# Last two tiles of the output in three token pieces, with 1 / rms from a square root and one Newton step

## The chip, the cores and the metric

The kernel runs on one core of one Trainium2 chip. The metric is the device time of one execution in microseconds (us), lower being better; the number that counts is the median over several runs. The core has five engines that run on their own and wait for one another by semaphores: TensorE (PE, with its weight loads shown apart as PEld), VectorE (DVE), ScalarE (ACT), GpSimd (POOL) and SyncE (SP), which here only issues DMAs. The profile is of one execution; "span" is the time from its first to its last instruction.

## The reference

One inference step of a two-layer decoder trunk on 544 tokens: 512 of a new sequence and 32 (8 sequences of 4) that continue from states. Layer 0 mixes tokens with a Mamba-2 recurrence, layer 1 with HGRN2; each is followed by a squared-ReLU MLP, and every sub-layer has an RMSNorm ahead of it. The change lies in the last lines of this:

```python
def rmsnorm(x, w):
    xf = x.astype(jnp.float32)
    y = xf * lax.rsqrt(jnp.mean(xf * xf, axis=-1, keepdims=True) + EPS)
    return (y * w.astype(jnp.float32)).astype(x.dtype)

def squared_relu_mlp(u, w_up, w_down):
    return jnp.square(jax.nn.relu(u @ w_up)) @ w_down
...
        h = h + squared_relu_mlp(rmsnorm(h, norm_mlp_w[layer]), mlp_w_up[layer], mlp_w_down[layer]).astype(h.dtype)
    y = rmsnorm(h, norm_f_w)
```

So the last thing computed is the down projection of the second MLP (4096 to 1024 channels), its addition to the residual, and the final norm, which needs for each token the sum of squares over all 1024 channels.

## The kernel before

**Layout.** Activations lie with channels on the 128 partitions and tokens along the free dimension: `x` is eight tiles of 128 channels by 544 tokens. [...] Weights are split into a high part (rounded to the type float32r) and a low part (the remainder), activations likewise, and a product of 128 channels by 128 channels is three matmuls: high by high, high by low, low by high. Each matmul instruction comes with its own weight load. A few small products work on plain float32; the trace shows two matmul instructions for each of them.

**The last MLP.** `mlp` goes through a list of units. Most of the down projection comes from a scheme that forms seven products instead of eight; the last two output tiles of the last quarter (channel tiles 6 and 7) are left over, and `finish` computes them together with the final norm. Its operands are `ops`, eight activation tiles split in high and low (`gh`, `gl`), and two units of weights `w` (`whi`, `wlo`), which `split` casts on ACT (L200) and subtracts on DVE (L201).

**What `finish` does,** for each half h of 272 tokens:

1. For tile 6 and then tile 7, 24 matmuls (8 operands, 3 each) into the half's bank of an accumulator (L1464, `pd`).
2. The sum is added to `x` on DVE (L1468), squared on ACT (L1469), and multiplied by the norm's weight column on DVE into `xw` (L1472). The squares of tiles 0 to 6 are gathered in `ssq` (L1474); tile 7's stay in `sq`.
3. The sums over channels: the tokens are cut in three chunks of 91 (the last overlaps), and each chunk of `ssq` and of `sq` is the stationary operand of a product with a column of ones (L1479, `fn_pc`). The result has tokens on partitions, 91 by 3.
4. `newton` (L351 to L363) on DVE: mean and epsilon (L1481), a first guess of 1 / sqrt from the bits of the float (L357), minus half the mean (L358), then three Newton steps of three instructions each (L360 to L362).
[...]
[...]

`newton` is also called by the other norms of the kernel (`rstd_steps`, and the HGRN2 heads); they call it without the new argument.

**What sets the order.** A planner in the compiler puts each engine's instructions in an order: among those that its own costs hold to be ready, the one that stands first in the program. So `fn_pc` and `fn_pr` of the first half stand in PE's queue between matmuls of the second half, and each engine then takes its queue strictly in that order, waiting where an operand is late. A DMA that ACT issues stands in ACT's queue and waits there for the `y` that it sends.

**Buffers.** [...] `f_pool` holds two buffers each of `sq`, `rb` and `y`. ACT evaluates functions from a table set that must be loaded first: the kernel warms it with an `Exp` of a small tile `warm` at its start.

Of the kernel before, what the change touches and what calls it, by code (L numbers as in the profile page):

```python
# [9 lines left out]
F32 = mybir.dt.float32  # L10
F32R = mybir.dt.float32r
I32 = mybir.dt.int32
AF = mybir.ActivationFunctionType
ALU = mybir.AluOpType
ADD, SUB, MUL, MAX, MIN = ALU.add, ALU.subtract, ALU.mult, ALU.max, ALU.min

P = 128
D = 1024
KT = D // P
# [3 lines left out]
HF = T // 2  # L23
SEQS = 8
EPS = 1e-5
# [79 lines left out]
def trunk(ctx: ExitStack, tc: tile.TileContext, io):  # L105
    nc = tc.nc
# [12 lines left out]
    x = [xa[:, k] for k in range(KT)]  # L119
    vec = const.tile([P, N_VEC], F32, name="vec")  # L120
    ident = const.tile([P, P], F32, name="ident")
    ones = const.tile([P, 2], F32, name="ones")
    nc.vector.memset(ones, 1.0)
    warm = const.tile([P, 2], F32, name="warm")
# [8 lines left out]
    ssq = const.tile([P, T], F32, name="ssq")  # L133
    nc.gpsimd.memset(ssq, 0.0)
    nt = ctx.enter_context(tc.tile_pool(name="nt", bufs=2))
# [183 lines left out]
    def block(w, c):  # L319

        return w[c // 512][:, c % 512 : c % 512 + P]
# [22 lines left out]
    def mx(name):  # L344
        return psm.tile([P, 512], F32, tag="mx", name=name)
# [2 lines left out]
        return t.rearrange("p (a b) -> p a b", a=2)  # L348


    def newton(ms, n):  # L351

        p = ms.shape[0]
        r = nt.tile([P, n], F32, tag="nwr", name="nwr")[:p]
        t = nt.tile([P, n], F32, tag="nwt", name="nwt")[:p]
        m = nt.tile([P, n], F32, tag="nwm", name="nwm")[:p]
        nc.vector.tensor_scalar(r.bitcast(I32), ms.bitcast(I32), -0.5, 1597463007.0, MUL, ADD)  # L357
        nc.vector.tensor_scalar(m, ms, -0.5, None, MUL)  # L358
        for _ in range(3):
            nc.vector.tensor_tensor(t, r, r, MUL)  # L360
            nc.vector.tensor_tensor(t, t, m, MUL)
            nc.vector.scalar_tensor_tensor(r, t, 1.5, r, ADD, MUL)  # L362
        return r  # L363

    def rstd_steps(scale, name, res, where, wait):

        pc = mx(f"{name}_pc")
        for c in range(5):
            c0 = min(c * P, T - P)
            nc.tensor.matmul(pc[:, c : c + 1], ssq[:, c0 : c0 + P], ones[:, 0:1], start=True, stop=True)  # L370
        ms = nt.tile([P, 5], F32, tag="ms", name=f"{name}_ms")
        nc.vector.tensor_scalar(ms, pc[:, :5], scale, EPS, MUL, ADD)
        r = newton(ms, 5)
        yield wait
        pr = mx(f"{name}_pr")
        pr2 = mx(f"{name}_pr2")
        for c in range(5):
            dst, w = (pr[:, c * P : (c + 1) * P], 0) if c < 4 else (pr2[:, :NS], P - NS)
            nc.tensor.matmul(dst, r[:, c : c + 1].to_broadcast([P, P]), ident[:, w:], start=True, stop=True)
        rb = where.tile([P, T], F32, tag="rb", bufs=1, name=f"{name}_rb")  # L380
        nc.scalar.copy(rb[:, :NP_], pr)
        nc.scalar.copy(rb[:, NP_:], pr2[:, :NS])
        res.append(rb)
# [30 lines left out]
    def weighted(k):  # L414
        xw.append(pers.tile([P, T], F32, tag=f"uh{k}", name=f"xw{k}"))
        return xw[k]
# [550 lines left out]
    def mlp(name, plan, v0, then, last=False):  # L967
# [158 lines left out]
        for x_ in plan:  # L1126
# [10 lines left out]
            elif x_[0] == "d":  # L1137
                _, u, k0, k1, m, q = x_
                if k0 == 0:
                    if q == 0 and m == 0:  # L1140
                        drain(name)
                        background(split_sums(), name, wait=2)
                    acc[m] = [acc_tile(f"pd{q}_{m}"), None]
                    if last and q == MLP_GROUPS - 1 and m >= KT - 2:
                        if m == KT - 2:
                            continue
                        ops = [g[u - 8 - m + i] for i in range(8)]
                        ws.close()
                        finish([unit(u - 1), unit(u)], ops, [acc[KT - 2][0], acc[m][0]])
                        continue  # L1150
                    acc[m][1] = unit(u)
                else:
                    ahead()
                ps, w = acc[m]
                gb = u - 8 - m
                products(ps, w, [g[gb + k] for k in range(k0, k1)], k0 == 0, k1 == 8, k0 * P)
                release((k0 < 4 <= k1) + (k1 == 8))
                if k1 == 8:
                    add_to_x(m, ps, then if q == MLP_GROUPS - 1 else None)
            else:  # L1160
                if queues[0] and queues[0][0][2] == name:
                    drain(name)
                seventh(*x_)
# [4 lines left out]
    def hgrn(then):  # L1168
# [151 lines left out]
        def states(h, d):  # L1320
# [41 lines left out]
            for c in range(4):  # L1362
# [12 lines left out]
            nc.vector.tensor_reduce(ms, o2, mybir.AxisListType.X, ADD)  # L1375
            nc.vector.tensor_scalar(ms, ms, 1.0 / P, EPS, MUL, ADD)
            r = newton(ms, 5)
            nc.vector.tensor_tensor(
                o2[:, :4], po.rearrange("p (a b) -> p a b", b=P), r[:, :4].unsqueeze(2).to_broadcast([P, 4, P]), MUL
# [68 lines left out]
                    add_to_x(2 * mp + i, ps, then if half == 1 else None)  # L1448
        es.close()

    CH = (0, 91, HF - 91)

    def finish(w, ops, pss):

        es = ExitStack()
        pool = es.enter_context(tc.tile_pool(name="f_pool", bufs=2, reuse_waits="tile"))
        ms2 = (KT - 2, KT - 1)
        for h in range(2):
            hs = slice(h * HF, (h + 1) * HF)
            sqs = []  # L1460
            for m, (hi, lo), ps in zip(ms2, w, pss):
                for k, (oh, ol) in enumerate(ops):
                    for j, (a, o) in enumerate(((hi, oh), (hi, ol), (lo, oh))):
                        nc.tensor.matmul(  # L1464
                            ps[:, h, :HF], block(a, k * P), o[:, hs], start=(k == 0 and j == 0), stop=(k == len(ops) - 1 and j == 2)
                        )
                sq = pool.tile([P, HF], F32, tag=f"sq{m}", name=f"sq{m}_{h}")
                nc.vector.tensor_tensor(x[m][:, hs], ps[:, h, :HF], x[m][:, hs], ADD)  # L1468
                nc.scalar.activation(sq, x[m][:, hs], AF.Square)  # L1469
                if h == 0:  # L1470
                    weighted(m)
                nc.vector.tensor_scalar(xw[m][:, hs], x[m][:, hs], vec[:, V_NF + m : V_NF + m + 1], None, MUL)  # L1472
                sqs.append(sq)
            nc.vector.tensor_tensor(ssq[:, hs], ssq[:, hs], sqs[0], ADD)  # L1474
            sq = sqs[1]
            pc = mx(f"fn_pc{h}")
            for n, c in enumerate(CH):
                for i, t in enumerate((ssq[:, hs], sq)):
                    nc.tensor.matmul(pc[:91, n : n + 1], t[:, c : c + 91], ones[:, 0:1], start=(i == 0), stop=(i == 1))  # L1479
            ms = nt.tile([P, 5], F32, tag="ms", name=f"fn_ms{h}")[:91, :3]  # L1480
            nc.vector.tensor_scalar(ms, pc[:91, :3], 1.0 / D, EPS, MUL, ADD)  # L1481
            r = newton(ms, 3)
            pr = mx(f"fn_pr{h}")
            for n, c in enumerate(CH):
                nc.tensor.matmul(pr[:, c : c + 91], r[:, n : n + 1].to_broadcast([91, P]), ident[:91, :91], start=True, stop=True)
            rb = pool.tile([P, HF], F32, tag="rb", name=f"fn_rb{h}")
            nc.scalar.copy(rb, pr[:, :HF])
            y = pool.tile([P, KT, HF], F32, tag="y", name=f"y{h}")
            for k in (0, 5, 1, 6, 2, 7, 3, 4):
                xk = xw[k][:, hs]  # L1490
                if k < 5:
                    nc.vector.tensor_tensor(y[:, k], xk, pr[:, :HF], MUL)
                else:
                    nc.gpsimd.tensor_tensor(y[:, k], xk, rb, MUL)
            for i, (k0, k1) in enumerate(((0, 2), (5, 7), (2, 5), (7, 8))):
                (nc.scalar if k0 >= 5 else nc.sync).dma_start(io["yT"][k0:k1, :, hs].rearrange("k p t -> p k t"), y[:, k0:k1])
        es.close()
# [117 lines left out]
def _build(arrays):  # L1615
    import concourse.bacc as bacc

    nc = bacc.Bacc("TRN2", target_bir_lowering=False, num_devices=1)
    io = {n: nc.dram_tensor(f"in_{n}", v.shape, mybir.dt.from_np(v.dtype), kind="ExternalInput").ap() for n, v in arrays.items()}
    for n, s in _OUT.items():  # L1620
        io[n] = nc.dram_tensor(f"out_{n}", s, F32, kind="ExternalOutput").ap()
    with tile.TileContext(nc) as tc:
        trunk(tc, io)
    return nc
# [22 lines left out]
```

## Time and profile before

| what | value |
|---|---|
| time, median of 3 runs | 1528.34 us (1526.07 to 1529.8) |
| the profiled execution's own time | 1524.65 us |
| its span | 1522.7 us |
| PE busy | 1503.0 us, 99% of the span |
| DVE, ACT, POOL busy | 1230.8, 842.2, 149.6 us |
| granted TensorE clock, mean | 0.995 of full |

The span is 1.95 us shorter than the time of the same execution; the rest lies outside the first and the last instruction. PE is busy almost throughout, and the only long stretch in which it isn't is the end: the last slice of the forty in the page's view of the span is the one with little PE work in it. A row of the timeline reads: start, duration, engine, line, operation, output from inputs, sizes (partitions by free elements), and in brackets how long the engine stood idle before it and who ended that.

### The profile page before, as it was taken

To read this page: it belongs to the slowest core of one execution; us is meant where nothing else is said; L and a number is where in the kernel's file an instruction comes from. 1 tells how busy PE (TensorE), PEld (TensorE's weight loads), DVE (VectorE), ACT (ScalarE), POOL (GpSimd) and SP (SyncE) were. 2 spreads that over 40 slices of the span, in tenths; PEclk is the share of its full clock that TensorE was granted. 3 is DMA by queue.
4 is the path that set the end of the run, shared out by engine and by line. 5 is a ranking of instruction groups with operands and counts; after the bars stand their busy time and mean duration, and the time that the engine had idled before them with its cause. 6 is when DMAs were issued, how large, how long until landed. Compare 5 with 4: busy or idle time off the path is not lost. (4 is left out here: it accounts for less than half of the span.)

```text
span 1522.7 us, 33053 instructions
## 1 busy us (share of the span) xinstructions
PE 1503.0 (99%) x13216; PEld 1447.0 (95%) x13216; DVE 1230.8 (81%) x2456; ACT 842.2 (55%) x1656; POOL 149.6 (10%) x229
## 2 busy tenths in 40 slices
PE   9999999999999999999999999999999999999997
PEld 7998989898999999999999999999999999999997
DVE  7889798978778649888898788888878749888896
ACT  5684766757355428576676333333335428576673
POOL 3211011110010001111110000000000001011101
PEclk9999999999999999999999999999999999999998
DMA  6476556574462237575754232233225327565741
GB/s 198 106 194 165 145 137 204 131 222 114 118 181 84 84 92 174 141 191 132 187 131 129 72 100 86 86 105 96 86 87 145 96 84 171 147 166 154 178 127 67
DMA packets 97722, 202.34 MB, mean 133 GB/s; under 512 B 15584, under 2 KB 35968, under 8 KB 97568
## 3 DMA queue, kind: packets, MB, share of 16 engines
q1 hardware_dynamic: 79600, 168.67, 35.1%
q0 software_dynamic: 16704, 30.42, 12.5%
q8 instruction: 104, 1.70, 0.5%
q10 hardware_dynamic: 1264, 1.14, 0.2%
q14 instruction: 50, 0.41, 0.1%
HBM read 183.01 MB, written 17.18 MB: 131 GB/s over the span
## 5 line engine op out<-in xcount | busy, mean ns | idle before, releaser
L200 ACT CAST whi<-raw 128x512 fp32r<-128x512 f32 x250 | 154.0, 618 | 293.6 <-PE ps L334 155.4
L201 DVE TENSOR_TENSOR wlo<-raw,whi 128x512 fp32r<-128x512 f32 x250 | 172.0, 689 | 57.4 <-ACT whi L200 54.5
L189 POOL DMA_DIRECT2D v<-in_W x82 | 71.8, 1024 | 665.8 <-DMA v<-in_W 215.1
L334 PE MATMUL ps<-uh_s,whi 128*128 128x272 f32 x576 | 125.3, 299 | 2.5 <-DVE BC L515 2.4
L334 PE MATMUL ps<-ul_s,whi 128*128 128x272 f32 x576 | 121.4, 292 | 0.0
L334 PE MATMUL ps<-uh,whi 128*128 128x272 f32 x512 | 112.6, 300 | 0.0
L334 PE MATMUL ps<-ul,whi 128*128 128x272 f32 x512 | 106.5, 289 | 0.0
L334 PE MATMUL ps<-uh,wlo 128*128 128x272 f32 x512 | 106.3, 289 | 0.0
L334 PEld LDWEIGHTS ps<-uh_s,whi 128*128 128x128 f32 x576 | 91.5, 191 | 8.5 <-issue 6.9
L334 PE MATMUL pd<-gh,whi 128*128 128x272 f32 x448 | 92.8, 289 | 0.0
L334 PE MATMUL pd<-gl,whi 128*128 128x272 f32 x448 | 92.7, 288 | 0.0
L334 PEld LDWEIGHTS ps<-ul_s,whi 128*128 128x128 f32 x576 | 92.0, 191 | 0.3
L334 PE MATMUL pd<-gh,wlo 128*128 128x272 f32 x448 | 91.9, 286 | 0.0
L334 PE MATMUL ps<-uh_s,wlo 128*128 128x272 f32 x576 | 86.1, 289 | 0.0
L334 PEld LDWEIGHTS ps<-uh,whi 128*128 128x128 f32 x512 | 80.8, 189 | 3.7 <-issue 1.4
L201 DVE TENSOR_TENSOR fl_p<-raw,fh_p 128x512 fp32r<-128x512 f32 x82 | 55.8, 688 | 30.6 <-ACT fh_p L200 28.8
L334 PEld LDWEIGHTS ps<-ul,whi 128*128 128x128 f32 x512 | 80.4, 189 | 0.0
L334 PEld LDWEIGHTS ps<-uh,wlo 128*128 128x128 f32 x512 | 80.0, 188 | 0.0
L334 PEld LDWEIGHTS ps<-uh_s,wlo 128*128 128x128 f32 x576 | 77.9, 189 | 1.1 <-issue 0.8
L200 ACT CAST fh_p<-raw 128x512 fp32r<-128x512 f32 x82 | 50.1, 619 | 39.8 <-PE pp L1080 17.9
L334 PEld LDWEIGHTS pd<-gl,whi 128*128 128x128 f32 x448 | 70.5, 188 | 0.0
L334 PEld LDWEIGHTS pd<-gh,wlo 128*128 128x128 f32 x448 | 70.4, 188 | 0.0
(472 smaller groups left out, 4825.9 us busy)
## 6 DMA issues: line engine op xcount, KB each, us to landing
raw<-in_W SPq DMA_DIRECT2D x181, 512.0 KB, 3.6
v<-in_W SPq DMA_DIRECT2D x82, 256.0 KB, 4.2
v<-in_W POOLq DMA_DIRECT2D x82, 256.0 KB, 5.5
a<-in_W SPq DMA_DIRECT2D x41, 256.0 KB, 4.5
wlo<-in_W POOLq DMA_DIRECT2D x34, 256.0 KB, 6.1
w<-cum_d SPq DMA_DIRECT2D x16, 512.0 KB, 6.8
st<-in_ssm_in SPq DMA_DIRECT2D x16, 512.0 KB, 4.7
out_ssm_s<-st SPq DMA_DIRECT2D x16, 512.0 KB, 6.6
```

The lines of the kernel that those rows point to most:

```text
L189: nc.gpsimd.dma_start(raw[:, c : c + 512], io["W"][u + 1][:, :512], accum_op=ADD)
L200: nc.scalar.copy(hi, raw)
L201: (eng or nc.vector).tensor_tensor(lo, raw, hi.bitcast(F32), SUB)
L334: nc.tensor.matmul(ps[:, h, :HF], block(a, c0 + k * step), o[:, h * HF : (h + 1) * HF], start=(first and i == 0), stop=(last and i == len( ...
```

## The change

Only `newton` and `finish` change.

- The tokens are taken in three pieces of 272, 176 and 96 columns in place of two of 272. The first two pieces use the two banks of the accumulators as before; the third has two banks of its own, `fl6` and `fl7`, taken from `psm` at the start of `finish`. Everything that was done once for each half is done once for each piece: 48 matmuls, the additions and squares, the sums, the reciprocal root, the spreading, eight `y` and four DMAs.
- The chunks of step 3 follow the piece: three of 91, two of 88, one of 96.
- 1 / rms: ACT takes the square root of the mean (`AF.Sqrt`), DVE its reciprocal, and one Newton step follows in place of three. An `AF.Sqrt` of `warm` stands at the head of `finish`.

```diff
-    def newton(ms, n):
+    def newton(ms, n, root=None):
 
         p = ms.shape[0]
-        r = nt.tile([P, n], F32, tag="nwr", name="nwr")[:p]
+        r = nt.tile([P, n], F32, tag="nwr", name="nwr")[:p] if root is None else root
...
-        nc.vector.tensor_scalar(r.bitcast(I32), ms.bitcast(I32), -0.5, 1597463007.0, MUL, ADD)
+        if root is None:
+            nc.vector.tensor_scalar(r.bitcast(I32), ms.bitcast(I32), -0.5, 1597463007.0, MUL, ADD)
+        else:
+            nc.vector.reciprocal(r, root)
         nc.vector.tensor_scalar(m, ms, -0.5, None, MUL)
-        for _ in range(3):
+        for _ in range(3 if root is None else 1):
...
-    CH = (0, 91, HF - 91)
+
+    PIECES = ((0, HF), (HF, 176), (HF + 176, 96))
 
     def finish(w, ops, pss):
...
-        for h in range(2):
-            hs = slice(h * HF, (h + 1) * HF)
+        nc.scalar.activation(warm, ones, AF.Sqrt)
+        last = [mx(f"fl{m}") for m in ms2]
+        for h, (c0, n) in enumerate(PIECES):
+            hs = slice(c0, c0 + n)
             sqs = []
-            for m, (hi, lo), ps in zip(ms2, w, pss):
+            for m, (hi, lo), ps_, pl in zip(ms2, w, pss, last):
+                ps = ps_[:, h, :n] if h < 2 else pl[:, :n]
...
+            nch = -(-n // P)
+            cw = -(-n // nch)
+            chs = [min(i * cw, n - cw) for i in range(nch)]
             pc = mx(f"fn_pc{h}")
-            for n, c in enumerate(CH):
-                for i, t in enumerate((ssq[:, hs], sq)):
-                    nc.tensor.matmul(pc[:91, n : n + 1], t[:, c : c + 91], ones[:, 0:1], start=(i == 0), stop=(i == 1))
-            ms = nt.tile([P, 5], F32, tag="ms", name=f"fn_ms{h}")[:91, :3]
-            nc.vector.tensor_scalar(ms, pc[:91, :3], 1.0 / D, EPS, MUL, ADD)
-            r = newton(ms, 3)
+            for i, c in enumerate(chs):
+                for j, t in enumerate((ssq[:, hs], sq)):
+                    nc.tensor.matmul(pc[:cw, i : i + 1], t[:, c : c + cw], ones[:, 0:1], start=(j == 0), stop=(j == 1))
+            ms = nt.tile([P, 5], F32, tag="ms", name=f"fn_ms{h}")[:cw, :nch]
+            nc.vector.tensor_scalar(ms, pc[:cw, :nch], 1.0 / D, EPS, MUL, ADD)
+            r0 = nt.tile([P, 5], F32, tag="nwr", name=f"fn_r{h}")[:cw, :nch]
+            nc.scalar.activation(r0, ms, AF.Sqrt)
+            r = newton(ms, nch, r0)
             pr = mx(f"fn_pr{h}")
...
```

The copies, the products and the DMAs behind it are as before, over n columns in place of 272.

More of the change, by code (lines that the diff above doesn't have):

```diff
@@ L1464, in finish @@
                         nc.tensor.matmul(
-                            ps[:, h, :HF], block(a, k * P), o[:, hs], start=(k == 0 and j == 0), stop=(k == len(ops) - 1 and j == 2)
+                            ps, block(a, k * P), o[:, hs], start=(k == 0 and j == 0), stop=(k == len(ops) - 1 and j == 2)
                         )
-                sq = pool.tile([P, HF], F32, tag=f"sq{m}", name=f"sq{m}_{h}")
-                nc.vector.tensor_tensor(x[m][:, hs], ps[:, h, :HF], x[m][:, hs], ADD)
+                sq = pool.tile([P, HF], F32, tag=f"sq{m}", name=f"sq{m}_{h}")[:, :n]
+                nc.vector.tensor_tensor(x[m][:, hs], ps, x[m][:, hs], ADD)
                 nc.scalar.activation(sq, x[m][:, hs], AF.Square)
@@ L1475, in finish @@
             sq = sqs[1]
+            nch = -(-n // P)
+            cw = -(-n // nch)
+            chs = [min(i * cw, n - cw) for i in range(nch)]
             pc = mx(f"fn_pc{h}")
-            for n, c in enumerate(CH):
-                for i, t in enumerate((ssq[:, hs], sq)):
-                    nc.tensor.matmul(pc[:91, n : n + 1], t[:, c : c + 91], ones[:, 0:1], start=(i == 0), stop=(i == 1))
-            ms = nt.tile([P, 5], F32, tag="ms", name=f"fn_ms{h}")[:91, :3]
-            nc.vector.tensor_scalar(ms, pc[:91, :3], 1.0 / D, EPS, MUL, ADD)
-            r = newton(ms, 3)
-            pr = mx(f"fn_pr{h}")
[L1484 to L1488, printed above, removed]
+            for i, c in enumerate(chs):
[6 more added lines that the diff above has]
+            r = newton(ms, nch, r0)
+            pr = mx(f"fn_pr{h}")
+            for i, c in enumerate(chs):
+                nc.tensor.matmul(
+                    pr[:, c : c + cw], r[:, i : i + 1].to_broadcast([cw, P]), ident[:cw, :cw], start=True, stop=True
+                )
+            rb = pool.tile([P, HF], F32, tag="rb", name=f"fn_rb{h}")[:, :n]
+            nc.scalar.copy(rb, pr[:, :n])
+            y = pool.tile([P, KT, HF], F32, tag="y", name=f"y{h}")[:, :, :n]
             for k in (0, 5, 1, 6, 2, 7, 3, 4):
@@ L1491, in finish @@
                 if k < 5:
-                    nc.vector.tensor_tensor(y[:, k], xk, pr[:, :HF], MUL)
+                    nc.vector.tensor_tensor(y[:, k], xk, pr[:, :n], MUL)
                 else:
```

## The prediction

> **What bounds the kernel now.** I read the page's first part, then the chain of work that ended last over the closing 30 us, then the timeline of the tail. The page:
>
> ```profile
> span 1522.7 us, 33053 instructions
> ...
> PE 1503.0 (99%) x13216; PEld 1447.0 (95%) x13216; DVE 1230.8 (81%) x2456; ACT 842.2 (55%) x1656; POOL 149.6 (10%) x229
> ```
>
> PE sets the time up to its last `pd` matmul; what comes behind it is a chain in which PE is nearly idle. The change touches the last 27 us only, so its effect is one of a few us either way. The chain in order of time (start, length, what), then the timeline:
>
> ```profile
> 1496.38 6.03 PE pd L1464 x48
> ...
> 1503.72 0.75 PE fn_pc L1479 x10
> ...
> 1506.62 0.92 PE fn_pr L1485 x6
> ```
>
> ```profile
> 1510.15 0.28 PE L1464 MATMUL pd<-gh,wlo 128*128 128x272 f32 x1
> ...
> 1510.47 0.44 DVE L1468 TENSOR_TENSOR x<-pd,x 128x272 f32<-128x272 f32 x1 [0.66 <-PE pd L1464]
> 1510.95 0.43 ACT L1469 ACTIVATE sq<-x 128x272 f32<-128x272 f32 x1 [3.00 <-DVE x L1468]
> ...
> 1511.43 0.32 PE L1479 MATMUL fn_pc<-ones,sq 128*91 128x1 f32 x2 [0.91 <-ACT sq L1469]
> ...
> 1512.10 0.30 PE L1479 MATMUL fn_pc<-ones,sq 128*91 128x1 f32 x2
> 1512.43 0.16 DVE L1481 TENSOR_SCALAR fn_ms<-fn_pc 91x3 f32<-91x3 f32 x1 [1.12 <-PE fn_pc L1479]
> ...
> 1512.83 0.16 DVE L360 TENSOR_TENSOR nwt<-nwr 91x3 f32<-91x3 f32 x1
> 1513.02 0.16 DVE L361 TENSOR_TENSOR nwt<-nwt,nwm 91x3 f32<-91x3 f32 x1
> ...
> 1514.57 1.17 PE L1485 MATMUL fn_pr<-ident,nwr 91*128 91x91 f32 x6 [2.18 <-DVE nwr L362]
> 1515.78 0.39 ACT L1487 COPY fn_rb<-fn_pr 128x272 f32<-128x272 f32 x1 [4.41 <-PE fn_pr L1485]
> 1516.20 1.83 DVE L1492 TENSOR_TENSOR y<-xw,fn_pr 128x272 f32<-128x272 f32 x5 [1.68 <-ACT fn_rb L1487]
> 1516.24 2.19 POOL L1494 TENSOR_TENSOR y<-xw,fn_rb 128x272 f32<-128x272 f32 x3 [5.91 <-ACT fn_rb L1487]
> 1517.01 0.37 SPq L1496 DMA_DIRECT2D out_yT<-y  x1
> ...
> 1518.47 0.34 ACTq L1496 DMA_DIRECT2D out_yT<-y  x1
> ```
>
> The last product ends at 1510.43, the span at 1522.7: a tail of 12.3 us. Each row starts as the one above it ends; nothing covers them. The stretches of 0.5 us show the rest (time, busy of PE, PEld, DVE, ACT, POOL, then clock, DMA share, GB/s):
>
> ```profile
> 1515.00:1515.50 0.50, 0.50 (x5) 0.50 (x3) 0.00 (x0) 0.00 (x0) 0.00 (x0) 0.56 0.00 0
> ...
> 1517.50:1518.00 0.50, 0.00 (x0) 0.00 (x0) 0.50 (x2) 0.00 (x0) 0.50 (x2) 0.50 0.15 52
> 1518.00:1518.50 0.50, 0.00 (x0) 0.00 (x0) 0.03 (x1) 0.00 (x0) 0.44 (x1) 0.50 1.04 359
> ...
> 1521.00:1521.50 0.50, 0.00 (x0) 0.00 (x0) 0.00 (x0) 0.00 (x0) 0.00 (x0) 0.50 0.10 31
> ```
>
> The output flows at 359 GB/s from about 1517.94 (0.93 us after SP's first issue) to 1521.04, which is the half's 1.11 MB (8 x 128 rows of 272 x 4 bytes); then 1.66 us pass to the span's end. `fn_pr` takes 1.17 us here against 0.92 in the first half, since the clock falls to 0.56 while it runs.
>
> **Term A: the matmuls of the second half (+4.7 us).** 48 of 272 columns take 6.03 us, 126 ns each. They become 96: 48 of 176 columns and 48 of 96. Each comes with its own weight load, and the question is which of the two sets the pace. No product of float32r in the trace is narrower than 272 columns. Rows that bound it:
>
> ```profile
> L1464 PEld LDWEIGHTS pd<-gh,whi 128*128 128x128 f32 x32 | 6.0, 189 | 0.0
> ```
>
> ```profile
> 824.88 1.28 PE L370 MATMUL hn_pc<-ones,ssq 128*128 128x1 f32 x10
> ```
>
> ```profile
> 102.04 1.05 PE L650 MATMUL pi<-BC,hT 128*128 128x128 f32 x8
> ```
>
> ```profile
> L370 PEld LDWEIGHTS hn_pc<-ones,ssq x10: 186/192/192, 824.9 to 825.9; 128*128 128x128 f32 x10
> ...
> L370 PE MATMUL hn_pc<-ones,ssq x10: 250/250/271, 824.9 to 825.9; 128*128 128x1 f32 x10
> ```
>
> ```profile
> L781 PE MATMUL pn<-xq,bm x32: 388/393/472, 130.9 to 411.6; 128*128 128x512 f32 x32
> ```
>
> ```profile
> L1464 PE MATMUL pd<-gh,whi x32: 282/288/372, 1496.2 to 1509.9; 128*128 128x272 f32 x32
> ```
>
> With one column, ten matmuls behind 128-column weights start (1.28 - 0.25) / 9 = 114 ns apart; with 128 columns eight start (1.05 - 0.28) / 7 = 110 ns apart. The width hardly matters: the weight load is the floor. Those loads are of float32 and last 192 ns; `pd`'s last 189. So I take 112 ns for every narrow `pd`: 96 x 0.112 = 10.75 us, and A = +4.7. Lower end, streaming alone: from 272 to 512 columns a matmul lengthens from 288 to 393 ns, 0.44 ns a column, so 126 ns falls to 84 at 176 and 49 at 96: 48 x 0.133 = 6.4 us, A = +0.4. Upper end: below, as a rival.
>
> [...]
>
> **Term B: one more set of sums and spreading ahead of the last product (+1.2).** Piece 1's `fn_pc` (eight, at 0.75 / 10 each, 0.6) and `fn_pr` (four, at 0.92 / 6, 0.6) stand between PE's matmuls. Piece 0 keeps its own. Whether PE waits for piece 1's root depends on where the planner puts `fn_pr`; I assume no wait beyond what the first half's group holds.
>
> **Term C: the tail (12.3 becomes 8.0, -4.3).** For 96 columns:
>
> ```profile
> L1271 DVE TENSOR_TENSOR T<-T 128x136 f32<-128x136 f32 x8 | 2.4, 295 | 0.0
> ...
> L1271 DVE TENSOR_TENSOR T<-T 128x64 f32<-128x64 f32 x8 | 1.7, 213 | 0.0
> ```
>
> ```profile
> L1196 DVE RECIPROCAL lb_den<-lb_p 128x8 f32<-128x8 f32 x1 | 0.2, 193 | 0.0
> ```
>
> ```profile
> L1343 ACT COPY S<-pS 128x128 f32<-128x128 f32 x8 | 2.1, 266 | 13.6 <-PE pS L1341 13.6
> ...
> L1413 ACT ACT_TABLE_LOAD x1 | 1.3, 1283 | 0.0
> ...
> L125 ACT ACTIVATE warm<-ones 128x2 f32<-128x2 f32 x1 | 0.2, 204 | 0.0
> ```
>
> - Addition 0.25 (between 213 and 295 ns), square 0.28 (0.43 less 176 x 0.83 ns, ACT's slope between 266 ns at 128 and 386 at 272 columns), three hand-overs of 0.04: 0.66 us, was 1.00.
> - Sums behind the square: 2 matmuls, not 10: 0.33, was 1.00.
> - Root: 0.20 for the mean, 0.24 for the square root (the 204 ns of a two-column activation and a hand-over; the trace has no Sqrt), 0.23 for the reciprocal, 3 x 0.19 for a step, 0.05: 1.28, was 2.14.
> - Spreading: 2 instructions at the full clock, 0.4, was 1.2; copy 0.24 + 0.04, was 0.42.
> - `y` and output, was 4.87 (1516.17 to 1521.04). DVE's five start 0.35 apart now and 0.17 then; the first pair is done 0.44 after the copy, data flow from 1.40. 0.39 MB at 359 GB/s is 1.1 us: 2.5 in all. But the 8 x 128 rows remain and shrink from 1088 to 384 bytes; if each costs as much as now they need 3.05 us: 4.45. No row separates small packets, so the middle, 3.45.
> - The closing 1.66 us stay.
>
> Sum 0.66 + 0.33 + 1.28 + 0.4 + 0.28 + 3.45 + 1.66 = 8.06 us.
>
> [...]
>
> **Covered at no cost.** The table load for `warm`'s Sqrt, 1.28 + 0.20 us on ACT. Behind it stand casts of tile 7's weights:
>
> ```profile
> 1498.53 0.60 ACT L200 CAST whi<-raw 128x512 fp32r<-128x512 f32 x1
> ...
> 1499.31 0.68 DVE L201 TENSOR_TENSOR wlo<-raw,whi 128x512 fp32r<-128x512 f32 x1
> ...
> 1500.99 0.29 PE L1464 MATMUL pd<-gh,wlo 128*128 128x272 f32 x1
> ```
>
> PE first needs this `wlo` at 1500.99, in tile 7's fifth product, and it is ready at 1499.99: 1.0 us of cover, so between 0 and +0.5. Piece 1's `y` and DMAs run under piece 2's 5.4 us of matmuls. The third use of `y` and `rb` takes piece 0's buffers, whose output lands during piece 2's matmuls at the latest. `fl6`, `fl7` leave two PSUM tiles for `fn_pc` and `fn_pr`, one for each, whose users are done a piece earlier.
>
> **Sum.** 4.7 + 1.2 - 4.3 = +1.6 us: 1526.3 for an execution like the profiled one (1524.65), which ran 3.7 us under the median. On the median, **1529.9 us**. Its own range: DMA -1.0 to +1.0, cast and PE waits up to +0.8, spacing 0.2: 1528.7 to 1531.9; the three runs scatter by 2 us: 1527 to 1533.5.
>
> **Rivals.**
>
> 1. *The weight load is no floor for float32r.* A = +0.4: net -2.7, **1525.6**. For it: the array takes float32 products in two instructions and float32r in one, so the loads may differ. Against: both loads last the same, 189 and 192 ns.
> 2. *Slower: narrow float32r products are done like float32, in two steps.* Place: L1464 in pieces 1 and 2; decided by a width somewhere between 272 and 176. Price: two steps of 112 ns for each of 96 products, 21.5 us, A = +15.5: net +12.4, **1540.7**. For it: every float32r product here is at least 272 wide. Against: the steps go by type wherever the trace shows them (float32 in two at 1 and at 128 columns).
> 3. *Piece 1's norm collides with the tail.* If the planner takes narrow matmuls for cheaper than they are, `fn_pr` of piece 1 lands near the end of piece 2's product. Then piece 1's copy, three POOL products (about 0.5 each) and two ACT DMAs (0.38 each) stand ahead of piece 2's square: about +2.5, **1532.4**. For it: before, the first half's two ACT issues ended 0.2 us ahead of the second half's square (1509.62 + 1.10 against 1510.95):
>
> ```profile
> 1509.62 1.10 ACTq L1496 DMA_DIRECT2D out_yT<-y  x2
> ```
>
>    Against: 5.4 us of matmuls against a chain of about 4.
> 4. *The Newton steps saved are spent on table loads,* if Square and Copy are not in Sqrt's set: two loads of 1.28 in the tail, more ahead: +2.6 to +5, about **1533.5**. Against: only two loads in the whole kernel, with Square and Copy after each.
>
> **Chances.** Forecast 0.67, rival 1 0.13, rival 2 0.07, rival 3 0.10, rival 4 0.03. A measurement of this kernel tells about 0.3%, 4.6 us, from no change. Faster by more: only rival 1 at the edge of the scatter, 0.05. Slower by more: rival 2, half of 3 and 4, and the forecast's upper edge: 0.15. Within: 0.80. Range: 1524.5 (rival 1) to 1535 (rivals 3 and 4).
>
> **What would show it.** Starts of `pd` in pieces 1 and 2: 110 to 114 ns apart right, 84 and 49 rival 1, 224 rival 2. The last `pd` ends about 5.9 us later in the span, and the tail behind it is 7 to 9 us. A third table load ahead of piece 0's Square and none later. A gain of over 3 us, or a loss of over 4, would make the sum wrong.

## The result and the profile after

The kernel as changed takes 1535.62 us in the median of six runs (1533.93 to 1541.58) beside 1526.60 us for the kernel before on the same chip (1524.64 to 1529.80). The ratio is 1.0067, with a 95% interval from 1.0054 to 1.0079: it is slower by about 9 us, where 1529.9 us was forecast. The profiled execution has a time of 1535.55 us and a span of 1533.8, 11.1 us above the span before.

The head of the page, as shown of before:

```profile
span 1533.8 us, 33185 instructions
...
PE 1513.3 (99%) x13264; PEld 1457.5 (95%) x13264; DVE 1232.3 (80%) x2460; ACT 846.7 (55%) x1666; POOL 150.1 (10%) x232
```

In the rows below, `fn_pr` is the product with the identity that brings 1 / rms back to tokens along the free dimension, and `fn_rb` is its copy by ACT; of the eight products `y` of a piece, which are `xw` times that result, five are DVE's and read `fn_pr`, and three are POOL's and read `fn_rb`. Of the four DMAs that send `y`, SP issues two and ACT two.

The closing part of the chain of waits (start, length, what):

```profile
1498.54 6.04 PE pd L1471 x48
...
1505.53 1.28 ACT L1494
...
1507.86 0.92 PE fn_pr L1498 x6
...
1512.01 0.36 ACT sq L1476
...
1515.37 0.68 PE fn_pr L1498 x4
1516.05 1.50 PE fl L1471 x12
```

Two things are new in it. The first product of the last two tiles starts at 1498.54 where it started at 1496.38, 2.16 us later, although nothing ahead of it was meant to change. And the chain leaves TensorE between the products of pieces 1 and 2. The timeline of the changed kernel shows that stretch, from piece 1's first product on:

```profile
1504.51 0.33 PE L1471 MATMUL pd<-gh,whi 128*128 128x176 f32 x1
...
1512.01 0.35 ACT L1476 ACTIVATE sq<-x 128x176 f32<-128x176 f32 x1 [2.82 <-DVE xw L1479]
...
1512.40 0.27 PE L1471 MATMUL pd<-gh,wlo 128*128 128x176 f32 x1
...
1512.71 0.34 DVE L1475 TENSOR_TENSOR x<-pd,x 128x176 f32<-128x176 f32 x1
...
1513.09 0.35 ACT L1476 ACTIVATE sq<-x 128x176 f32<-128x176 f32 x1 [0.73 <-DVE x L1475]
...
1513.49 0.32 PE L1490 MATMUL fn_pc<-ones,sq 128*88 128x1 f32 x2 [0.38 <-ACT sq L1476]
...
1515.37 0.68 PE L1498 MATMUL fn_pr<-ident,fn_r 88*128 88x88 f32 x4 [1.25 <-DVE fn_r L365]
1515.84 0.29 PE L1471 MATMUL fl<-gh,whi 128*128 128x96 f32 x1
...
1516.41 0.28 PE L1471 MATMUL fl<-gh,wlo 128*128 128x96 f32 x1
1516.52 0.28 PE L1471 MATMUL fl<-gh,whi 128*128 128x96 f32 x1
...
1517.09 0.41 PE L1471 MATMUL fl<-gl,whi 128*128 128x96 f32 x1
1517.31 0.41 PE L1471 MATMUL fl<-gh,wlo 128*128 128x96 f32 x1
```

The planner put piece 1's whole norm ahead of piece 2's first `fl` in TensorE's queue, so from 1512.67 to 1515.4 TensorE does little but wait: for tile 7's addition and square, and then for the root. Tile 6's square is late as well (it stands behind the issue of a DMA on ScalarE, which waits for piece 0's `y`; ScalarE is idle for 2.82 us ahead of it), but this costs next to nothing: tile 7's addition starts at 1512.71, 0.04 us after the last product of piece 1 ends. When the `fl` products begin they start 110 ns apart, and from 1517 on 215 ns apart. The table by stretches (time, busy of PE, PEld, DVE, ACT, POOL, then clock, DMA share, GB/s) says why, and shows the output of the last piece:

```profile
1516.50:1517.00 0.50, 0.50 (x6) 0.50 (x5) 0.50 (x3) 0.00 (x0) 0.50 (x2) 0.83 0.00 0
1517.00:1517.50 0.50, 0.50 (x4) 0.50 (x4) 0.50 (x4) 0.00 (x0) 0.50 (x2) 0.50 0.00 0
...
1524.50:1525.00 0.50, 0.50 (x5) 0.50 (x4) 0.00 (x0) 0.00 (x0) 0.00 (x0) 0.50 0.00 0
...
1530.50:1531.00 0.50, 0.00 (x0) 0.00 (x0) 0.00 (x0) 0.00 (x0) 0.00 (x0) 0.50 0.92 221
1531.00:1531.50 0.50, 0.00 (x0) 0.00 (x0) 0.00 (x0) 0.00 (x0) 0.00 (x0) 0.50 1.07 288
```

The clock granted to TensorE falls to 0.50 and stays there through the other 39 or so products, although TensorE is busy without a break. The tail behind them:

```profile
1524.98 0.41 PE L1471 MATMUL fl<-gh,wlo 128*128 128x96 f32 x1
...
1525.20 0.44 PE L1490 MATMUL fn_pc<-ones,ssq 128*96 128x1 f32 x2
...
1526.12 0.48 PE L1490 MATMUL fn_pc<-ones,sq 128*96 128x1 f32 x2 [0.48 <-ACT sq L1476]
1526.64 0.15 DVE L1492 TENSOR_SCALAR fn_ms<-fn_pc 96x1 f32<-96x1 f32 x1 [0.64 <-PE fn_pc L1490]
...
1527.94 0.71 PE L1498 MATMUL fn_pr<-ident,fn_r 96*128 96x96 f32 x2 [1.34 <-DVE fn_r L365]
...
1529.07 0.91 DVE L1507 TENSOR_TENSOR y<-xw,fn_pr 128x96 f32<-128x96 f32 x5 [1.28 <-ACT fn_rb L1502]
```

From the end of the last product (1525.39) to the end of the span are 8.41 us, against 12.3 before. So the tail did shrink by 3.9 us; what ate it and 11 us more lies ahead of it.

### The profile page after: what moved, and what is told of

Same layout as the page of the kernel before. It is cut to its first block, busy times and chain, and to the rows that moved or that the text cites. A ratio compares the mean times of both kernels' runs of the same rounds, so it can differ in the third digit from the quotient of the medians.

```text
span 1533.8 us, 33185 instructions
## 1 busy us (share of the span) xinstructions
PE 1513.3 (99%) x13264; PEld 1457.5 (95%) x13264; DVE 1232.3 (80%) x2460; ACT 846.7 (55%) x1666; POOL 150.1 (10%) x232
```

## The experiments

Each kernel was timed against the kernel before on the same chip. Two theories stood at the start (not the terms of the prediction that have the same letters): A, that the early Sqrt at the head of `finish` costs the body some 2 us beside what the pieces cost; B, that it costs nothing and all of the loss is that of the narrow pieces, by TensorE's wait and its clock.

**1. One part of the change alone.** The pieces without the new root (the bit guess and three steps stay); the new root with two halves of 272; and the whole change without the early Sqrt.

```diff
-        nc.scalar.activation(warm, ones, AF.Sqrt)
...
-            r0 = nt.tile([P, 5], F32, tag="nwr", name=f"fn_r{h}")[:cw, :nch]
-            nc.scalar.activation(r0, ms, AF.Sqrt)
-            r = newton(ms, nch, r0)
+            r = newton(ms, nch)
```

> The three pieces alone: the old root (bit guess and three Newton steps), no square root anywhere. Theory A (the loss has two places: the Sqrt of the small tile, which the planner drew forward to 7 us and which costs about 2 us at the start, and the pieces at the end): two table loads in all, the first matmul of the last two tiles at about 1496 to 1497 us as before, piece 2 at half the clock, the root 0.86 us longer in the tail and in TensorE's wait ahead of piece 2; so after less 2 plus 1.5: +8 to +9 us on before. Rival B (the early square root is innocent and the late start is scatter): +10 to +11.

Measured: 1543.41 us (1540.09 to 1544.03) beside 1525.58, ratio 1.0112, interval 1.0097 to 1.0127. More than either theory allowed.

```diff
-    PIECES = ((0, HF), (HF, 176), (HF + 176, 96))
+    PIECES = ((0, HF), (HF, HF))
```

> The new root alone, with two halves of 272: square root, reciprocal, one Newton step, and the Sqrt of the small tile. Theory A: five table loads, one at 7 us, start of the last two tiles about 2 us late, tail 0.9 us shorter: +1 us on before. Rival B: -0.9. Should the granted clock at 10 to 20 us stay at 1.00, the 2 us are smaller.

Measured: 1527.27 us (1526.54 to 1528.54), ratio 1.0008, interval 0.9999 to 1.0018: 1.7 us above before, on A's side, though the interval still holds 1.

```diff
-        nc.scalar.activation(warm, ones, AF.Sqrt)
```

> The changed kernel without its Sqrt of the small tile; the table is then loaded at the first root, as it is in the changed kernel anyway. Theory A: three table loads, start of the last two tiles as before, the end as in the changed kernel: about +7 us on before. Rival B: +9 like the changed kernel.

Measured: 1537.90 us (1533.57 to 1539.11), ratio 1.0075, interval 1.0058 to 1.0092; not below the changed kernel's 1535.62, on B's side. Experiment 3 shows why these two don't agree.

Most of the loss is the pieces' and not the root's. Of the pieces with the old root, the timeline shows the clock falling still earlier, inside piece 1. The longer root makes TensorE wait 1.3 us for piece 0's `fn_pr`, and from 1510.1 on every stretch is at 0.50 until the end: 176-column products that start 112 ns apart at the full clock start 215 apart.

```profile
1506.83 0.28 PE L1470 MATMUL pd<-gl,whi 128*128 128x176 f32 x1
...
1508.42 0.90 PE L1495 MATMUL fn_pr<-ident,nwr 91*128 91x91 f32 x6 [1.31 <-DVE nwr L365]
```

The table by stretches of the same run (TensorE's busy time and count, clock, DMA share, GB/s):

```profile
1510.50:1516.00 5.50, 5.50 (x27) 0.50 0.59 203
```

**2. Piece 2 with wide matmuls.** Its 48 products stream all 272 columns of the second half; only the last 96 are used.

```diff
-                ps = ps_[:, h, :n] if h < 2 else pl[:, :n]
+                ps = ps_[:, h, :n] if h < 2 else pl[:, HF - n : HF]
+                out, cols = (ps, hs) if h < 2 else (pl[:, :HF], slice(HF, T))
...
-                            ps, block(a, k * P), o[:, hs], start=(k == 0 and j == 0), ...
+                            out, block(a, k * P), o[:, cols], start=(k == 0 and j == 0), ...
```

> The changed kernel, but the 48 matmuls of piece 2 stream all 272 columns of the second half and only the last 96 of their result are used (176 columns are computed twice). Theory C1 (TensorE's idle stretch around piece 1's root lowers the clock, about 4 us later, and narrow matmuls then keep it low): the clock falls within the first 2 us of piece 2 as before and comes back to 1.00 some 3 to 4 us after; piece 2's product takes 6 us plus 2 to 3 for the slow stretch, 8 to 9 us against 9.3 in the changed kernel. Theory C2 (narrow matmuls alone lower the clock, idle or not): no fall, 6.0 us.

Measured: 1533.12 us (1530.85 to 1538.96), ratio 1.0059, interval 1.0040 to 1.0077. Streaming nearly three times the columns is no slower than streaming 96. The table by stretches of this run (TensorE alone):

```profile
1514.00:1517.00 3.00, 2.37 (x10) 0.50 0.01 2
1517.00:1520.00 3.00, 3.00 (x15) 0.50 0.76 240
1520.50:1523.50 3.00, 3.00 (x26) 1.00 0.00 0
```

The clock fell at 1513.5, with TensorE's wait, and came back at 1520.4; piece 2's product took 8.3 us, as theory C1 has it. Under 96-column matmuls it never came back in 8 us. That left two readings: the wait makes it fall and narrow matmuls only keep it down, or they push it down by themselves.

**3. No wait between the pieces.** Piece 2's products are issued ahead of piece 1's norm. Beside it the Sqrt's table is loaded late: the Sqrt reads `ssq`, so that it can't be drawn to the start. And both together.

```diff
+        s0 = product(0, *PIECES[0])
+        norm(0, *PIECES[0], s0)
+        s1 = product(1, *PIECES[1])
+        s2 = product(2, *PIECES[2])
+        norm(1, *PIECES[1], s1)
+        norm(2, *PIECES[2], s2)
```

> The changed kernel with the products of piece 2 issued ahead of piece 1's norm, so that TensorE runs from piece 1's product into piece 2's without the 2.7 us of near idleness. Theory I (the idle stretch is what makes the clock fall; narrow matmuls only keep it from rising again): the clock stays 1.00 through piece 2's product, 48 x 111 ns = 5.4 us, and about 2.7 + 3.9 us go, of which piece 1's norm and y behind it give back up to 2: 1529 to 1531 us. Theory T (matmuls bound by the load of weights count as idle themselves): the clock falls within some 4 us of piece 1's or piece 2's narrow matmuls all the same, the product takes 7 us or more, and the time is 1532 to 1534 us.

Measured: 1532.26 us (1530.79 to 1540.90), ratio 1.0054, interval 1.0031 to 1.0076. Its runs lie at two levels, four at 1530.8 to 1532.3 and two at 1539.5 and 1540.9. The profiled one is of the upper level; in it the clock falls at 1508.4, in the midst of piece 1:

```profile
1504.50:1507.90 3.40, 2.77 (x26) 1.00 0.00 0
1508.50:1514.50 6.00, 6.00 (x30) 0.50 0.56 190
1515.00:1525.00 10.00, 10.00 (x50) 0.50 0.00 0
```

Six us of 176 columns without a break, then ten of 96, and the clock does not rise. My theory that the wait between the pieces is the cause, and would be worth 4 to 6 us in all runs, fell.

```diff
-        nc.scalar.activation(warm, ones, AF.Sqrt)
+        nc.scalar.activation(warm, ssq[:, 0:2], AF.Sqrt)
```

> The changed kernel with the early Sqrt made to read ssq, so that it can't be drawn to the start. Theory W: the two loads at 7.4 and 47.5 us and the load inside piece 0's root go, so the first product starts at 1496.4 again (1.4 us sooner at an equal clock) and piece 0's root is 1.28 us shorter; the stretch of idleness ahead of piece 2 and the half clock behind it stay: 1533 to 1534 us. Theory N (the load's place is worth nothing): 1535.6 us.

Measured: 1539.97 us (1533.64 to 1542.45, four runs), ratio 1.0083, interval 1.0054 to 1.0112.

> Both: piece 2's products ahead of piece 1's norm, and the late Sqrt. Theories I and W together: 1527.5 to 1529 us with a clock of 1.00 through piece 2's product. Theory T: 1531 us or more, the clock at half in piece 2's product.

Measured: 1540.44 us (1532.85 to 1541.39, four runs), ratio 1.0081, interval 1.0056 to 1.0106.

The first median lies above what either theory gave, the second on theory T's side. Both kernels are at the upper level in three runs of four, and both profiled executions show the clock falling inside piece 1, at 1507.5 and 1508.8. Two levels are seen in the changed kernel too: it has four runs at 1533.9 to 1535.7 (mean clock 0.991 to 0.992) and two at 1539.7 and 1541.6 (0.987). A gain of 1 or 2 us from the Sqrt's place can't be read from medians that jump by 6.

It can be looked for in the traces. The body ahead of the last two tiles has its own lapses to half clock (0.50), 3.4 us each (one of 6.8 in the pieces with the old root), which differ from run to run; two executions are comparable where these agree. Before, the kernel with late Sqrt, the two halves with early Sqrt and the kernel of experiment 2 (early Sqrt) each have two of them, between 150 and 170 us:

```profile
1496.41 6.04 PE pd L1471 x48
```

```profile
1497.80 6.03 PE pd L1470 x48
```

```profile
1497.80 6.04 PE pd L1472 x48
```

The first line is of the chain with the late Sqrt (before: 1496.38), the others are those with the early one: 1.4 us later. That is the largest gap, and not the typical one: a later kernel with the early Sqrt (the narrow one of experiment 4) also starts at 1496.41, with lapses at other places. A point ahead of the lapses at 150 us is a fairer mark. The first product of tile `pi` (layer 0), at 102.04 us before, starts at 101.76 to 102.43 in the eight profiled executions without an early Sqrt and without a lapse by then, and at 102.64 to 103.23 in the four with one: 0.9 us later in the mean, between 0.2 and 1.5 singly.

The timeline of ScalarE in the changed kernel shows the place:

```profile
7.36 1.28 ACT L1462 ACT_TABLE_LOAD   x1
...
8.76 0.60 ACT L200 CAST whi<-raw 128x512 fp32r<-128x512 f32 x1
```

The Sqrt depends on nothing but a constant, so the planner drew it from the end of the program to 7.36 us, in front of a cast of the first layer's weights; TensorE waited 1.65 us for that cast, until 9.42. A second load of 1.28 us, ahead of a Tanh, follows at 47.5 us. After one more at 834.06, which the kernel before has as well (at 831.89), the last stands in the root of piece 0, 1.28 us from 1505.53; it ends 0.1 us after the mean that the root needs.

**4. The width alone.** In one more kernel without the wait, pieces 1 and 2 both stream 272 columns.

> As the kernel with piece 2's products ahead of piece 1's norm, but pieces 1 and 2 both stream all 272 columns of the second half (only their 176 and 96 are used), 2 x 48 matmuls of 126 ns. Theory S (the clock falls for want of streamed columns, a matmul of 176 or 96 columns in a slot of 111 ns is a partly idle array): the clock stays 1.00 from the first product to the end of piece 2's, pieces 1 and 2 take 6.05 us each, and the runs have one level, 1530 to 1532 us, without the second one near 1540. Theory G (the stall and the small matmuls of piece 0's norm make it fall, whatever the width): the clock falls near 1508 us as with narrow matmuls in part of the runs, and the runs show two levels.

Measured: 1529.71 us (1528.70 to 1532.99), ratio 1.0030, interval 1.0018 to 1.0042: one level, and the clock is 1.00 until 1520, behind the last product. But the planner had moved piece 0's `fn_pr` in it, which took a small wait out. So I made a pair with that removed from both: `fn_pr` of piece 0 behind all of piece 1's products. TensorE then runs from early in piece 1 (1503.4) to the end of piece 2 without a wait, and the two kernels differ in the number of columns and, since the planner reckons with it, in whether 4 or 9 products stand ahead of piece 0's last five sums.

```diff
-        norm(0, *PIECES[0], s0)
+        r0 = norm(0, *PIECES[0], s0)
         s1 = product(1, *PIECES[1])
+        spread(0, *PIECES[0], *r0)
         s2 = product(2, *PIECES[2])
-        norm(1, *PIECES[1], s1)
-        norm(2, *PIECES[2], s2)
+        spread(1, *PIECES[1], *norm(1, *PIECES[1], s1))
+        spread(2, *PIECES[2], *norm(2, *PIECES[2], s2))
```

> The changed kernel, with piece 0's spreading matmuls (fn_pr) behind all of piece 1's product, and piece 2's product ahead of piece 1's norm: TensorE has 96 narrow matmuls in a row and waits for nothing between them. [...] Theory G (TensorE's waits and the small matmuls of the norm are needed to make it fall): the clock is 1.00 until the last narrow matmul, and the time is 1528 to 1530 us in all runs.

> The same program with 272 columns streamed by each matmul of pieces 1 and 2 (176 and 96 of them used). Both theories: the clock is 1.00 until the last of them, and they take 2 x 6.05 us, 1.5 us more than 96 x 111 ns; 1529 to 1531 us in all runs. Under theory S it is faster than the narrow form although it streams more; under G it is 1 to 2 us slower than the narrow form.

Measured: narrow 1532.35 us (1530.06 to 1534.91), ratio 1.0048, interval 1.0033 to 1.0063; wide 1530.15 us (1528.22 to 1532.55), ratio 1.0031, interval 1.0018 to 1.0044. The medians differ by 2.2 us and the intervals overlap, so the time alone does not settle it. The table by stretches does, first narrow, then wide:

```profile
1505.00:1509.00 4.00, 4.00 (x38) 1.00 0.01 4
1510.00:1514.00 4.00, 4.00 (x39) 1.00 0.44 153
1514.50:1515.50 1.00, 1.00 (x7) 0.51 0.95 328
```

```profile
1505.00:1509.00 4.00, 4.00 (x36) 1.00 0.01 4
1511.00:1515.00 4.00, 4.00 (x35) 1.00 0.39 133
1515.00:1517.00 2.00, 2.00 (x19) 1.00 0.84 295
```

In the narrow form the 176-column matmuls held the full clock while nothing interrupted them. The 96-column ones begin at 1509.84, and at 1514.5, 4.7 us on, the clock falls while TensorE is busy all the time. In the wide form it doesn't. The other runs agree: the mean clock is 0.992 or 0.993 in all five narrow ones and 0.994 to 0.997 in the six wide ones. So for 96 columns the clock fell without any wait, which is theory S's side (want of streamed columns) and not theory G's. For 176 columns it is less clear. The clock fell inside piece 1 in four profiled executions, all with two waits of TensorE for piece 0's norm there, of 0.39 us and of 0.25 to 1.31. The narrow kernel has only the first of them, and none of its five runs is at the upper level. But the profiled execution of the changed kernel has both waits, of 0.39 and 0.25 us, and held the full clock through piece 1. So an interruption may be needed and is not enough; what else decides is not shown.

**5. What the root is worth, and a better cut.** Two halves with the new root and no Sqrt ahead; with the late Sqrt; pieces of 288 and 256 with the late Sqrt; the same with the old root.

```diff
-    PIECES = ((0, HF), (HF, HF))
+    PIECES = ((0, 288), (288, 256))
```

> Two halves of 272 with the new root and without the early Sqrt. In the run of the new root with the early Sqrt the first product of the last two tiles starts 1.42 us later than before at the same clock (1497.64 against 1496.22 us), and the part behind it is 1.6 us longer because x's add stands ahead of Newton's step in VectorE's queue. Theory W (the early Sqrt costs the body 1.4 us by its load and the load back to Tanh's table): that 1.4 us goes, 1525.9 us beside 1525.6 of before, and the part behind stays 1 to 2 us too long. Theory N (the body's shift is chance): 1527.3 us, as with the early Sqrt.

> Two halves of 272, the new root, the Sqrt's table loaded late (it reads ssq), so that the load lies ahead of the first half's x and not inside its root. The planner then puts the first half's fn_pr after 10 matmuls behind its fn_pc and Newton's step ahead of x's add. If the new root's shorter chain (2.14 to 1.28 us, at 1513 us) is worth its length on the path: 1524.7 us beside 1525.6 of before. If the chain's gain is eaten elsewhere (the first half's y, the output's rate): 1525.6 us.

> The same with pieces of 288 and 256 columns: both wider than the floor of the weight load (111 ns, 240 columns at 0.46 ns), so TensorE's sum is the same 48 x 252 ns, and the last piece needs 2 chunks and not 3. Theory F (only columns below the floor cost TensorE time, and the tail shrinks with the piece): 0.3 to 1 us below the two halves of 272, 1523.7 to 1524.4 us. Rival (an uneven cut disturbs the planner's order or the clock): not below the two halves.

> Pieces of 288 and 256 with the old root (bit guess and three steps). If the gain of the 288 and 256 kernel with the new root (1.0 us in the median) comes from the cut alone: 1524.5 us here too. If it comes from the root: 1525.5 us. If from both, half each: 1525.0 us.

Measured, in this order: 1526.60 us (ratio 1.0004, interval 0.9995 to 1.0014), 1527.24 (1.0005, 0.9996 to 1.0013), 1524.52 (0.9991, 0.9982 to 1.0000) and 1525.13 (0.9996, 0.9987 to 1.0005). The first lies midway between theories W and N; the second lies above both values that were expected. Only 288 and 256 with the late Sqrt is below the kernel before by as much as 1 us, and the interval just touches 1; by the ratios it is some 11 us below the changed kernel. With the old root the same cut is 0.5 us below, well inside the noise. The root's shorter chain shows no gain by itself: in the two halves 0.9 us less than before was expected, and none came. There the traces show it eaten on both sides of the root. From the end of the last product to the mean pass 4.0 us (early Sqrt), 3.3 (none) and 2.4 (late) where 2.0 passed before, because the first half's `y` or DMA issues now stand ahead of the second half's additions and squares in their queues; and `fn_pr` takes 1.6 us at half clock where it took 1.17.

With 288 and 256 the traces show where the gain goes, too. From the mean to `fn_pr` the new root takes 1.23 us (1513.16 to 1514.39) and the old one 2.18 (1512.48 to 1514.66), and `y` starts that much sooner behind the last product. Yet both spans end 12.1 us behind it, for in the execution with the new root the output trails. Its table by stretches (the last two columns are DMA share and GB/s):

```profile
1520.50:1521.00 0.50, 0.00 (x0) 0.00 (x0) 0.00 (x0) 0.00 (x0) 0.00 (x0) 0.50 0.32 103
1521.00:1521.50 0.50, 0.00 (x0) 0.00 (x0) 0.00 (x0) 0.00 (x0) 0.00 (x0) 0.50 0.06 8
1521.50:1522.00 0.50, 0.00 (x0) 0.00 (x0) 0.00 (x0) 0.00 (x0) 0.00 (x0) 0.50 0.01 2
```

Such packets trail by about 0.9 us in two of the three executions of two halves with the new root as well (none and late Sqrt), and neither in the third nor with the old root. Why is open, so what the root is worth stays open between 0 and 1 us.

## Why the prediction was wrong, step by step

The prediction's sum gave +1.6 us of span; the profiled execution has +11.1. The 9.5 us between them, in order of time (the rows add up to 9.35; the rest is rounding):

| where | us | how |
|---|---|---|
| body ahead of the last two tiles | +2.16 | 1498.54 - 1496.38 |
| piece 0's norm inside piece 1 | +0.73 | 1504.51 to 1512.51 less 48 x 0.112, 2.62; before 1502.35 to 1510.27 less 6.03, 1.89; TensorE now waits 0.39 and 0.25 in it |
| TensorE's wait for piece 1's norm | +2.13 | 1512.51 to 1515.84, 3.33, less the 1.2 of Term B |
| half clock in piece 2 | +3.98 | 1515.84 to 1525.20, 9.36, less 48 x 0.112 |
| tail | +0.35 | 8.41 less 8.06 |

**Term A, right at the full clock, and then overtaken.** The 176-column and the first 96-column products start 110 to 112 ns apart, as taken from the float32 rows. Between 96 and 176 columns the width makes no difference; this agrees with the weight load as the floor, and rival 1 (no floor), whose estimate was 49 and 84 ns, is out. Rival 2 (two steps) is out as well: the 215 ns later on resemble its 224, but the weight loads lengthen with them, from 190 to 333 ns, and the clock reads 0.50. What Term A lacked is that half a clock nearly doubles the floor, from 111 to 215 ns.

**Term B is the step that failed.** "I assume no wait beyond what the first half's group holds": piece 1's norm had no product left to stand behind but piece 2's, and the planner did not put it there. Rival 3 saw a collision of that norm, in the other direction (too late, not too early). The wait costs 2.1 us. The prediction read the clock at 0.56 in the tail before as a detail of `fn_pr`; that TensorE's clock could fall ahead of the last product was in no term and no rival, and it costs 4.0 us in the profiled execution. The runs of the upper level take about 6 us more; the three executions of that level that were profiled, all of other kernels in experiment 3, have the fall inside piece 1. With these waits and the clock ahead of it, the last product ends 15.0 us later in the span, where 5.9 were forecast.

**Covered at no cost: wrong, by place.** The prediction reckoned the Sqrt's load where the program text has it, beside tile 7's casts. It ran at 7.36 us. By the mark at 102 us the loads cost the body about 0.9 of the 2.16 us. Most of the rest, 1.1 us by the same mark, goes with one more lapse of the clock, at 11.5 to 15 us, which needs no early Sqrt: the profiled execution of experiment 1 without it has that lapse as well, and the two halves with it do not. Of the signs named, "a third table load ahead of piece 0's Square and none later" was wrong twice: there are five loads, and the last one is in piece 0's root.

**Term C, right to 0.35 us, in part by luck.** By its parts: addition and square 0.67 (0.66 forecast), sums 0.54 (0.33), root 1.34 (1.28), spreading 0.76 (0.40), copy 0.32 (0.28), `y` and output 2.93 (3.45, between 2.5 and 4.45), the close 1.85 (1.66). The two largest shortfalls are TensorE's, at half clock; sums, spreading and close were 0.76 short in all, and the 0.52 to spare in `y` and output made up for most of it. The output of 384-byte rows flows at 221 to 288 GB/s where 1088-byte rows had 359. So the small rows do cost, yet less than in proportion: the rate is 0.62 to 0.80 of what it was, the row 0.35. Why is not shown.

## What to carry to other kernels

Cutting the last piece of a product smaller shortens the tail (here by 3.9 us), and costs TensorE nothing only as long as its matmuls stay wider than the weight load (here about 240 columns, an estimate: products start 111 ns apart at 96 and 176 columns, 118 at 256 and 133 at 288, so 0.46 ns a column above the floor); below that each cost the same here, and the cut adds products instead of moving them. A stream of matmuls far below that width did not hold the clock here (96 columns: from 1.00 to 0.51 after 4.7 us), although TensorE was busy throughout: check the clock in the last stage, and leave work to stand in TensorE's queue behind every chain that it must wait for. An instruction meant to warm something up needs a data dependence that holds it in place; without one a planner may move it over the whole program (here its load ran at 7.36 us, and at 1499.19 with `ssq` as the input).

## What the runs showed of the hardware that was not expected

- **Busy was not enough for the clock.** TensorE at 100% busy with 96-column float32r matmuls, one in 111 ns, lost its clock 4.7 us after they began. By the slope of Term A, 0.44 ns a column, such a matmul streams for 42 of its 111 ns, the 272-column one for 120 of its 126 (both estimates). At half clock neither 96 columns (10 us) nor 176 (5.5 and 6 us) brought it back; 272 columns brought it back 6.8 us after the fall and 4.9 us after the first of them, TensorE having waited for part of the time before. Why streamed columns should count is not shown; the runs show the width and the clock. Nor is it shown what the body's lapses of 3.4 us come from, or why their places differ between runs.
- **One program, two times.** The runs of the changed kernel lie at two levels some 6 us apart, 1533.9 to 1535.7 and 1539.7 to 1541.6 us. Its profiled execution is of the lower level and has the fall in piece 2 (1516.8); the three executions of an upper level that were profiled, of other kernels, have it in piece 1 (1507.5 to 1508.8). A median of few runs then says little of an edit worth 1 us.
- **Streaming unused columns need not cost time.** The pair of experiment 4 shows 1530.15 us with 272 columns a matmul and 1532.35 with 176 and 96, and experiment 2 1533.12 beside the changed kernel's 1535.62. The intervals overlap in both, so a gain is likely and not shown; no loss was seen.
